# mLSTM scores with queries on the partitions, both directions summed ahead of one value product per block

## The chip, the cores and the metric

The kernel runs on one core of a Trainium2 chip. The metric is the time of one execution in microseconds on the device. The engines are named as in the profile: PE is TensorE (matmuls; PEld are its weight loads), DVE is VectorE, ACT is ScalarE, POOL is GpSimd, and SP is the engine that issues most DMAs.

## The reference

One layer of an encoder block over 512 tokens of width 1024. Three token mixers work side by side on the normed input: a bidirectional mLSTM, a 2-D neighbourhood attention and a cross-attention into a memory. Their outputs are gated, summed and projected, and a gated feed-forward network follows. The change touches the mLSTM alone: 4 heads of width 128, both directions, summed and then normed.

```python
def mlstm_chunkwise(q, k, v, i_pre, f_pre):   # one direction
    ...
    causal = jnp.tril(jnp.ones((L, L), dtype=bool))
    D = a[..., :, None] - a[..., None, :] + log_i[..., None, :]
    D = jnp.where(causal, D, -jnp.inf)
    inter_log = a + m_prev[..., None]
    m_j = jnp.maximum(inter_log, jnp.max(D, axis=-1))
    qk = jnp.einsum('bhcjd,bhcsd->bhcjs', q, k)
    P = jnp.exp(D - m_j[..., None]) * qk
    inter_w = jnp.exp(inter_log - m_j)
    num = jnp.einsum('bhcjs,bhcsd->bhcjd', P, v) + inter_w[..., None] * jnp.einsum('bhcde,bhcje->bhcjd', C_prev, q)
    den = jnp.sum(P, axis=-1) + inter_w * jnp.einsum('bhce,bhcje->bhcj', n_prev, q)
    h = num / jnp.maximum(jnp.abs(den), jnp.exp(-m_j))[..., None]
    return h.reshape(B, H, S, Dh)
...
    h = h_fw + h_bw
    h = h * lax.rsqrt(jnp.mean(h * h, axis=-1, keepdims=True) + EPS)
```

So each direction has its own score matrix `P`, its own denominator and its own inter-block term from the state `C_prev`; the two directions share `qk` and `v`.

## The kernel before

The 512 tokens lie in four blocks of 128 (J = 0 to 3, one chunk of the recurrence each). Weights come from memory as float32 in blocks of 128x1024 (`emit_raw`, on SP's queue, three blocks ahead), are split by ACT (high part, L195) and DVE (low part, L196) into two reduced-precision parts one block ahead (`emit_split`), and each projection is three accumulating matmuls (`mm3`, L213 to L215). A projection of one 128-wide output tile is 24 such passes of 512 columns.

The mLSTM is a generator (`ml_all`, which begins with `ml_prep`) that is stepped in between the projections of other branches: `paced` steps it inside a projection, `step` behind one. `late` holds pieces of work that the next `flush` (in a projection) emits. The order in which instructions then stand on each engine's queue is decided at build time by a scheduler that goes by its own estimates of when inputs are ready; each engine runs its queue in that order.

`ml_prep` computes gates and the running maxima by scans along the tokens, writes one row per head and direction to memory (`rd`) and makes small per-token tables: `bi` and `mh` (exponents), `wt` and `dec` (state weights and decays), `em` (the floor of the denominator), `sc` (the inter-block weight). Per head, `load_R` then loads the two rows back, spread over all partitions (`R`, 128x512 for each direction), `mask` adds the causal mask to them, and the exponential of `R` plus a per-partition column is the decay matrix.

Per head h the stages are:

- `keys`: four transposes of the keys (L681), split into parts; `weigh` multiplies the values by the state weights (L700 to L704).
- `states`: state products of the four blocks (L722 and `mm3`), decayed sums `C` for both directions (L736).
- `edges`: the inter-block term of J = 0 (backward) and J = 3 (forward), which enters as a query scaled by its decay (L673, L675).
- `weights_J`: scores of a block with keys on the partitions (L748), two exponentials (L752), one product `E` for both directions (L753).
- `values_J`, one block later: two value products, one for each direction, with a column of constants in `va` that gives the denominators (L761); for J = 0 and 3 the edge product accumulates into the same PSUM tile (L763), for J = 1 and 2 a 258-wide `mm3` gives the inter-block term of both directions. Then come the denominators (L772 to L779) and the sum of the directions into `H` (L780 to L785), and its squares (L787).
- `normalise`: the power -0.5 on POOL (L793), four scalings by ACT (L798); `emit_y`: four transposes (L806) and the output gate.

The mLSTM stage and what stands beside it end in the merge of the first branch; behind the last transposes of head 3 the cross-attention, the neighbourhood attention, the output projection and the feed-forward network follow.

## Time and profile before

| what | value |
|---|---|
| median of 3 runs | 875.06 us (874.84 to 875.43) |
| the profiled execution's own time | 874.76 us |
| its span, first to last instruction | 873.0 us |
| granted TensorE clock, mean | 0.999 |
| instructions | 12227 |
| first and last key transposes (L681) | 115.7 and 197.4 us |
| last transposes of `emit_y` (L806) | 236.0 us |

In rows of the profile, a line like `L753 DVE TENSOR_TENSOR E<-E,at ...` names the source line, the engine, the operation, and output and inputs by the program's names. In groups, the count is followed by the busy time in us, the mean of one in ns, and the idle time of the engine ahead of it with what ended it. In the timeline the first column is the start and the second the duration, both in us; an idle time ahead of the instruction and its releaser stand in brackets. In windows each engine has its busy time and count, then follow the granted clock, the DMA share and GB/s.

### The profile page before, as it was taken

The page shows a single profiled execution, that of the slowest core. Times are in us where ns is not written, and L with a number is a line of the kernel's source. Part 1 is how long each engine was busy: PE and PEld are TensorE (multiplying, and loading weights), DVE is VectorE, ACT ScalarE, POOL GpSimd, SP SyncE. Part 2 cuts the span into 40 slices and gives each one's busy share as a digit, 9 for nine tenths or more (in the row PEclk, how much of TensorE's full clock was granted, in tenths as well). Part 3 has the DMA queues.
Part 4 walks back from the last instruction along what each step waited for, and adds up shares of the span by engine and source line. Part 5 has one row for each costly group of instructions (what it writes and reads, how often), then busy time and mean ns, then how long its engine had stood idle before and what let it go on. Part 6 is the DMA issues. An engine that isn't in the chain of part 4 may idle for free.

```text
span 873.0 us, 12227 instructions
## 1 busy us (share of the span) xinstructions
PE 867.6 (99%) x4303; PEld 735.9 (84%) x4303; DVE 593.4 (68%) x1240; ACT 470.7 (54%) x996; POOL 125.0 (14%) x201
## 2 busy tenths in 40 slices
PE   9999999999999999999999999999999999999997
PEld 7898889888888888888888888888888888888887
DVE  7794789886577768897676558776633466666534
ACT  7563567765455658898544455444422344444532
POOL 0101100000163370600000002111100011111010
PEclk9999999999999999999999999999999999999999
DMA  8324634522253453633233432332233332322412
GB/s 281 100 79 153 204 122 124 169 82 99 83 143 74 118 151 109 158 121 121 98 97 109 145 108 97 97 97 96 76 100 105 107 98 97 98 96 90 136 40 97
DMA packets 39421, 99.81 MB, mean 114 GB/s; under 512 B 5688, under 2 KB 13880, under 8 KB 39360
## 3 DMA queue, kind: packets, MB, share of 16 engines
q1 hardware_dynamic: 31568, 92.32, 33.3%
q0 software_dynamic: 7360, 6.32, 3.5%
q8 instruction: 34, 0.56, 0.3%
q10 hardware_dynamic: 432, 0.39, 0.1%
q14 instruction: 27, 0.22, 0.1%
HBM read 94.80 MB, written 4.21 MB: 113 GB/s over the span
## 4 chain that ended last, share of the span: by engine, by line
PE 98%; DVE 1%; issue 0%; ACT 0%; POOL 0%; POOLq 0%
PE mm L213 29%; PE mm L214 29%; PE mm L215 29%; PE at L214 2%; PE at L213 2%; PE at L215 2%; PE at L938 1%; PE at L761 1%; PE at L919 1%; PE at L900 0%; PE at L901 0%; PE at L748 0%; PE at L1026 0%; PE at L243 0%; PE mm L422 0%
## 5 line engine op out<-in xcount | busy, mean ns | idle before, releaser
L213 PE MATMUL mm<-u,wh 128*128 128x512 f32 (+1 forms) x1072 | 415.0, 387 | 0.0
L215 PE MATMUL mm<-u,wl 128*128 128x512 f32 (+1 forms) x1072 | 411.8, 384 | 0.0
L214 PE MATMUL mm<-u,wh 128*128 128x512 f32 (+1 forms) x1072 | 411.6, 384 | 0.0
L195 ACT ACTIVATE wh<-wr 128x512 fp32r<-128x512 f32 (+2 forms) x298 | 183.7, 621 | 207.1 <-PE mm L214 163.7
L196 DVE TENSOR_TENSOR wl<-wr,wh 128x512 fp32r<-128x512 f32 (+3 forms) x300 | 203.6, 681 | 89.8 <-ACT wh L195 86.7
L215 PEld LDWEIGHTS mm<-u,wl 128*128 128x128 f32 x1072 | 201.4, 188 | 40.2 <-DVE wl L196 0.2
L213 PEld LDWEIGHTS mm<-u,wh 128*128 128x128 f32 x1072 | 201.5, 188 | 38.6 <-ACT wh L195 0.2
L214 PEld LDWEIGHTS mm<-u,wh 128*128 128x128 f32 x1072 | 201.6, 188 | 38.2
L1374 POOL TENSOR_TENSOR s<-s,rb 128x512 f32<-128x512 f32 x22 | 38.2, 1735 | 402.6 <-DVE s L1373 238.9
L542 POOL DMA_DIRECT2D u<-nav_d x128 | 62.3, 511 | 67.2 <-PE at L938 22.7
L219 ACT ACTIVATE u<-s 128x512 fp32r<-128x512 f32 x26 | 16.4, 632 | 57.9 <-DVE s L1377 56.2
L1377 DVE TENSOR_TENSOR s<-mm,s 128x512 f32<-128x512 f32 x22 | 15.2, 690 | 23.8 <-POOL s L1374 23.8
L462 ACT ACTIVATE s<-pad,vec 128x512 f32<-128x512 f32 x30 | 24.4, 813 | 9.7 <-DVE pad L460 9.7
L220 DVE SCALAR_TENSOR_TENSOR u<-s,u 128x512 fp32r<-128x512 f32 x26 | 19.0, 732 | 14.8 <-ACT u L219 14.7
L463 DVE SCALAR_TENSOR_TENSOR s<-pad,vec,s 128x512 f32<-128x512 f32 x30 | 22.5, 750 | 5.5 <-ACT s L462 5.5
L1373 DVE SCALAR_TENSOR_TENSOR s<-s,s 128x512 f32<-128x512 f32 x22 | 15.2, 691 | 13.4 <-ACT s L1372 13.3
L464 DVE SCALAR_TENSOR_TENSOR s<-pad,vec,s 128x512 f32<-128x512 f32 x30 | 22.5, 750 | 0.8
L1372 ACT ACTIVATE s<-s 128x512 f32<-128x512 f32 x22 | 13.9, 632 | 14.9 <-DVE s L1371 14.9
L460 DVE TENSOR_TENSOR pad<-mm,rb 128x512 f32<-128x512 f32 x22 | 15.1, 690 | 6.5 <-PE mm L215 6.4
L1384 DVE TENSOR_TENSOR u<-mm,u 128x512 f32<-128x512 f32 x13 | 9.0, 691 | 14.6 <-PE mm L215 14.6
L213 PE MATMUL mm<-wh,u 128*128 128x512 f32 x48 | 18.8, 392 | 0.0
L214 PE MATMUL mm<-wl,u 128*128 128x512 f32 x48 | 18.7, 390 | 0.0
(341 smaller groups left out, 1051.5 us busy)
## 6 DMA issues: line engine op xcount, KB each, us to landing
wr<-wflat SPq DMA_DIRECT2D x141, 512.0 KB, 3.4
nab<-nabias SPq DMA_DIRECT2D x16, 256.0 KB, 2.7
u<-nav_d POOLq DMA_DIRECT2D x128, 32.0 KB, 2.8
s<-xT SPq DMA_DIRECT2D x15, 256.0 KB, 4.0
wr<-wflat SPq DMA_DIRECT2D x14, 192.0 KB, 2.4
nav_d<-nv POOLq DMA_DIRECT2D x8, 256.0 KB, 3.7
R<-rd SPq DMA_DIRECT2D x8, 256.0 KB, 5.4
wr<-wflat SPq DMA_DIRECT2D x2, 544.0 KB, 3.4
```

The source lines that it names most:

```text
L195: A.activation(h[:, u:v], src, AF.Copy)
L196: V.tensor_tensor(l[:, u:v], src, h[:, u:v].bitcast(F32), op=ALU.subtract)
L213: PE.matmul(ps, lh, rh, start=start, stop=False)
L214: PE.matmul(ps, lh, rl, start=False, stop=False)
L215: st["mm"] = PE.matmul(ps, ll, rh, start=False, stop=stop).ins
L219: A.activation(h, src, AF.Copy, scale=scale)
L220: V.scalar_tensor_tensor(l, src, scale, h.bitcast(F32), op0=ALU.mult, op1=ALU.subtract)
L462: A.activation(t1, pad[:, 0:512], AF.Identity, scale=vcol(w, i), bias=vcol(b, i))
L463: V.scalar_tensor_tensor(t1, pad[:, 1:513], vcol(w, n + i), t1, op0=ALU.mult, op1=ALU.add)
L464: V.scalar_tensor_tensor(t1, pad[:, 2:514], vcol(w, 2 * n + i), t1, op0=ALU.mult, op1=ALU.add)
L542: G.dma_start(vw[r * 32:(r + 1) * 32, i * 256:(i + 1) * 256], nav_v[hf, r, CW[b]:CW[b] + 32, hp * 256:(hp + 1) * 256])
L1374: G.tensor_tensor(c, c, rb2, op=ALU.mult)
```

## The change

The scores are computed with queries on the partitions, so that a denominator is a column. For each block the two decay matrices are multiplied by the scores with a row sum (`tensor_tensor_reduce`), whose start value is the inter-block part of the denominator; each direction's matrix is then divided by its denominator, the two are added, the sum is transposed on PE and copied to SBUF, and one product with the values follows. The inter-block numerators are scaled and written to `H` ahead of that, and the product is added to them. J = 0 and 3 take their inter-block term from a plain product of the queries with the state, and `edges` is gone. The table `br` replaces `bi` and `mh` in the exponent, `num` holds the two factors that the reciprocals are multiplied by, and the row written to `rd` is another one, which is ready earlier. A block now passes through three steps (`weights_J`, `turn_J`, `values_J`), held in `open_J`; `exps` computes the next block's exponentials at the end of `weights_J`. The key transposes use the projections' PSUM pool. One yield of `ml_prep` goes, and one is added at the end of head 3.

```diff
+        num = cp.tile([P, 2, 2, 4, 4], F32, name="num")
+        with tc.issue_after(st["pool"]):
+            G.memset(num, 1.0 / C_ML)
...
         A.activation(mr[64:100], cu[:36], AF.Copy)
-        yield
         rr = scr()
         rd = dp.tile([2, 4, S], F32, name="rd")
-        yield
-        V.tensor_tensor(rr[:36], cu[:36], mr[:36], op=ALU.subtract)
+        V.tensor_tensor(rr[:36], pl[64:100, :], cu[:36], op=ALU.subtract)
         for d in range(2):
             G.dma_start(rd[d], rr[32 * d:32 * d + 4, :])
+        yield
         yield
...
+            br = cp.tile([P, 2, 4, 4], F32, name="br")
+            sc = [num[:, 1, 0, 1:4], num[:, 1, 1, 0:3]]
             for d in range(2):
...
+                V.tensor_tensor(br[:, d], lfc[:, :, 64 + 32 * d:68 + 32 * d], lfc[:, :, 32 * d:32 * d + 4], op=ALU.subtract)
+                V.tensor_tensor(sc[d], br[:, d, 1 - d:4 - d], mh[:, d:d + 3, d, :], op=ALU.add)
...
-            V.tensor_tensor(r4, r4, msk[d].unsqueeze(1).to_broadcast([P, 4, P]), op=ALU.add)
-
-        def edges(h, R, ee):
-            ...
+            V.tensor_tensor(r4, r4, msk[1 - d].unsqueeze(1).to_broadcast([P, 4, P]), op=ALU.add)
 
         def keys(h, R, ee):
-            pt = atps()
+            pt = mmps()
...
+        def exps(h, J, R):
+            W = tp.tile([P, 4, P], F32, tag="E", name=nm("E"))[:, 0:2, :]
+            for d in range(2):
+                with tc.issue_after(st["act"]):
+                    A.activation(W[:, d, :], R[d][:, J * P:(J + 1) * P], AF.Exp, bias=ml["br"][:, d, J, h:h + 1])
+            ahead.append(W)
+
+        def weights_J(H, ss, h, J, k, w, C, q, R, ee):
+            num, W = ml["num"], ahead.pop()
             js, hs = slice(J * P, (J + 1) * P), slice(h * S + J * P, h * S + (J + 1) * P)
+            ds = (1,) if J == 0 else (0,) if J == NT - 1 else (0, 1)
             ps = atps()
             kq = ps[:, 384:512]
-            PE.matmul(kq, kT[:, hs], qT[:, hs], start=True, stop=True)
+            PE.matmul(kq, qT[:, hs], kT[:, hs], start=True, stop=True)
+            if len(ds) == 2:
+                qs = slice((J - 1) * P, J * P)
+                mm3(ps[:, :258], q[0][:, qs], q[1][:, qs], w[1][J - 1], w[2][J - 1], True, True)
+            else:
+                d = ds[0]
+                PE.matmul(ps[:, 129 * d:129 * d + 129], qT[:, hs], C[d][J - 1 + d], start=True, stop=True)
+            pi = ps[:, :258].rearrange("p (d c) -> p d c", d=2)
+            E = ee[:, J % 2 * 256:J % 2 * 256 + 256].rearrange("p (x c) -> p x c", x=2)
+            y = tiny(8)
+            init, den, r = y[:, 0:2], y[:, 2:4], y[:, 4:8].rearrange("p (x d) -> p x d", x=2)
+            dd = slice(ds[0], ds[-1] + 1)
+            V.tensor_tensor(init[:, dd], pi[:, dd, 128], num[:, 1, dd, J, h], op=ALU.mult)
             for d in range(2):
...
+                V.tensor_tensor_reduce(W[:, d, :], W[:, d, :], kq, C_ML, init[:, d:d + 1] if d in ds else 0.0,
+                                       ALU.mult, ALU.add, accum_out=den[:, d:d + 1])
             emv = em[:, J, :].rearrange("p (a b) -> p a b", b=4)
+            V.scalar_tensor_tensor(den, den, -1.0, den, op0=ALU.mult, op1=ALU.max)
             V.tensor_tensor(den, den, emv[:, 0:9:8, h], op=ALU.max)
             V.reciprocal(den, den)
...
+            V.tensor_tensor(r, num[:, :, :, J, h], den.unsqueeze(1).to_broadcast([P, 2, 2]), op=ALU.mult)
+            A.activation(E[:, 0, :], W[:, 0, :], AF.Copy, scale=r[:, 0, 0:1])
+            V.scalar_tensor_tensor(E[:, 0, :], W[:, 1, :], r[:, 0, 1:2], E[:, 0, :], op0=ALU.mult, op1=ALU.add)
+            src = None
+            for d in ds:
+                if src is None:
+                    A.activation(H[:, js], pi[:, d, 0:128], AF.Copy, scale=r[:, 1, d:d + 1])
+                else:
+                    V.scalar_tensor_tensor(H[:, js], pi[:, d, 0:128], r[:, 1, d:d + 1], src, op0=ALU.mult, op1=ALU.add)
+                src = H[:, js]
+            if J < NT - 1:
+                exps(h, J + 1, R)
+            return H, ss, h, J, E, ps
+
+        def turn_J(H, ss, h, J, E, ps):
+            pt = ps[:, 384:512]
+            PE.transpose(pt, E[:, 0, :], ident)
+            A.activation(E[:, 1, :], pt, AF.Copy)
+
+        def values_J(H, ss, h, J, E, ps):
+            js = slice(J * P, (J + 1) * P)
+            pv = ps[:, 384:512]
+            PE.matmul(pv, E[:, 1, :], va[:, J, h, 0:128], start=True, stop=True)
+            V.tensor_tensor(H[:, js], pv, H[:, js], op=ALU.add)
             sq = scr(128)
             A.activation(sq, H[:, js], AF.Square, accum_out=ss[:, J:J + 1])
...
         for h in range(4):
             if prev:
-                values_J(h - 1, 3, *E, *own, *prev)
-                normalise(*prev)
+                values_J(*open_J.pop(0))
+                turn_J(*open_J[0])
             states(h, *st_h)
...
+            exps(h, 0, R)
+            yield
+            if prev:
+                values_J(*open_J.pop(0))
+                normalise(*prev)
+            last = prev
+            prev = tp.tile([P, S], F32, tag="H", name=nm("H"), bufs=4), tiny(4)
+            open_J.append(weights_J(*prev, h, 0, *own))
             yield
             for J in range(1, NT):
...
+                if J > 1:
+                    values_J(*open_J.pop(0))
+                turn_J(*open_J[0])
+                if J == 2 and last:
+                    emit_y(h - 1, last[0])
+                open_J.append(weights_J(*prev, h, J, *own))
                 if J == 3 and h < 3:
-                    st_h = keys(h + 1, *nxt)
+                    st_h = keyed(h + 1)
+                if J < 3 and h < 3:
+                    late.append(lambda d=J - 1, n=nxt: mask(n, d))
                 yield
...
```

In the built order of the new kernel, `weigh` is at L694 to L698, the state products at L716, the scores at L750, the inter-block product of J = 0 and 3 at L756, the reduce at L764, the scaling at L771 and the combination at L772, the transpose at L786 and its copy at L787, the value product at L792 and the addition at L793, the four scalings of `normalise` at L806, the masks at L670. The norm of the memory (L337 to L341), with two table loads on ACT, and the `o` projections run beside head 0 in both kernels.

More of the change, by code (lines that the diff above doesn't have):

```diff
@@ L615, in ml_prep @@
         em = cp.tile([P, NT, 36], F32, name="em")
-        cp.tile([P, NT, 38], F32, name="gap2")
+        cp.tile([P, NT, 30], F32, name="gap2")
         A.activation(lfc, pmv, AF.Copy)
@@ L708, in keys, with states @@
             late.append(weigh)
-            return (ke, kh, kl), (ew, wh, wl), C, q, eq, R
-        def states(h, k, w, C, q, eq, R):
+            return (ke, kh, kl), (ew, wh, wl), C, q, R, ee
+        def states(h, k, w, C, q, R, ee):
             flush()
@@ L740, in states @@
                 split_act(wh[j], wl[j], tj[j][:, :258])
-        def weights_J(h, J, R):
-            bi = ml["bi"]
+        def exps(h, J, R):
+            W = tp.tile([P, 4, P], F32, tag="E", name=nm("E"))[:, 0:2, :]
+            for d in range(2):
+                with tc.issue_after(st["act"]):
[3 more added lines that the diff above has]
+            num, W = ml["num"], ahead.pop()
@@ L814, in ml_all, with keyed @@
         prev = None
-        E = None
-        def load_head(h):
-            return load_R(h), tp.tile([P, S], F32, tag="H", name=nm("ee"), bufs=4)
-        nxt = load_head(0)
-        st_h = keys(0, *nxt)
+        open_J, ahead = [], []
+        def keyed(h):
+            return keys(h, nxt, tp.tile([P, S], F32, tag="H", name=nm("ee"), bufs=4))
+        nxt = load_R(0)
+        st_h = keyed(0)
         yield
```

70 lines of the change are left out of this document (9 added, 61 removed).

## The prediction

> **What bounds the kernel now.** I read the page first: the busy shares, the slices, the chain that ended last.
>
> ```profile
> span 873.0 us, 12227 instructions
> PE 867.6 (99%) x4303; PEld 735.9 (84%) x4303; DVE 593.4 (68%) x1240; ACT 470.7 (54%) x996; POOL 125.0 (14%) x201
> DVE  7794789886577768897676558776633466666534
> PE 98%; DVE 1%; issue 0%; ACT 0%; POOL 0%; POOLq 0%
> ```
>
> TensorE is the bound from end to end, so the time falls only by passes taken off PE and rises only by waits put into PE's queue. The mLSTM heads run between about 110 and 236 us, interleaved with projections; there DVE is the second busiest, so I looked at that stretch by windows (columns: PE, PEld, DVE, ACT, POOL).
>
> ```profile
> 110.00:120.00 10.00, 10.00 (x52) 8.43 (x51) 9.84 (x32) 6.58 (x17) 1.03 (x2) 1.00 0.24 67
> 120.00:130.00 10.00, 10.00 (x51) 8.45 (x51) 7.43 (x20) 7.43 (x23) 0.00 (x0) 1.00 0.62 199
> 130.00:140.00 10.00, 10.00 (x54) 8.53 (x54) 9.24 (x30) 9.17 (x22) 0.84 (x1) 1.00 0.23 75
> 140.00:150.00 10.00, 10.00 (x78) 9.65 (x77) 9.02 (x28) 6.65 (x18) 0.00 (x0) 1.00 0.54 144
> ```
>
> PE has no hole here, but DVE is busy 35.5 of 40 us: head 0 has little room for more DVE work or for a DVE that waits.
>
> **PE's passes.** Records overlap, so I go by starts in the timeline of PE.
>
> ```profile
> 131.67 0.39 PE L215 MATMUL mm<-u,wl 128*128 128x512 f32 x1
> 131.90 0.38 PE L748 MATMUL at<-u,u 128*128 128x128 f32 x2
> 132.12 0.61 PE L761 MATMUL at<-u,E 128*128 128x129 f32 x4
> 132.56 0.39 PE L763 MATMUL at<-C,ee 128*128 128x129 f32 x2
> 142.24 0.60 PE L681 MATMUL at<-ident,u 128*128 128x128 f32 x4
> 142.68 0.61 PE L761 MATMUL at<-u,E 128*128 128x129 f32 x4
> ```
>
> A 512-wide pass takes 0.23 us (131.67 to 131.90). Plain float32 products are two passes each: L761 is two matmuls and x4 here, 0.44 us to the next start, 0.11 per pass. The four transposes L681 are x4, one pass each, also 0.44. Per head and block the old code has scores (2 passes) and two value products (4); the new has scores (2), one transpose (1), one value product (2). The inter-block products keep their number: the 258-wide triple for J = 1, 2 and one float32 product for J = 0, 3. That is 6 against 5 passes: 16 x 0.11 = **1.78 us off PE**. The built order of PE agrees: summed over its passes, the stretch from the transposes of the running maxima to the last transpose of head 3 is 1.78 us shorter, and everything after it is the same sequence. By "TensorE: Matmul & The Clock Gate", Part 4, in the Trainium skill, a 128x128 transpose costs about 275 ns within a kernel; the records do last 272 ns, but the starts here are 0.11 apart, and by the rule 16 x 0.275 = 4.4 against the 3.55 of the passes dropped would be an estimated loss of 0.85.
>
> **DVE and ACT.** Rows by shape, between 110 and 245 us:
>
> ```profile
> L753 DVE TENSOR_TENSOR E<-E,at 128x256 f32<-128x256 f32 x16 | 6.6, 413 | 1.2 <-PE at L748 1.2
> L781 DVE SCALAR_TENSOR_TENSOR H<-at,y,H 128x128 f32<-128x128 f32 x16 | 5.6, 347 | 3.2 <-ACT H L780 3.1
> L779 DVE RECIPROCAL y<-y 128x2 f32<-128x2 f32 x16 | 2.6, 161 | 0.3
> L327 DVE CUSTOM_DVE_ANT_0 s<-at,ident 128x128 f32<-128x128 f32 x2 | 0.6, 282 | 0.0
> L327 DVE DVE_READ_ACCUMULATOR2_ANT y<- 128x1 f32 x2 | 0.2, 82 | 0.0
> ```
>
> Per head DVE loses four L753 (1.65), eight H updates (2.78), fourteen tiny operations at about 0.16 (2.2) and the edge product (about 0.41): 7.0. It gains eight multiply-and-reduce pairs (8 x 0.364 = 2.9), twenty tiny ones (3.2), six 128-wide combinations (2.1) and four additions, between a tiny 0.16 and 0.35, say 0.28 (1.1): 9.3. So +2.3 per head, 9 in all, and about 3 in the four windows above: 38.5 of 40. That fits, just. ACT loses two edge exponentials and four tiny Abs per head and gains four scaled copies and four PSUM copies, about +1. None of this is on PE's path by itself; what counts is the path from a block's scores to its transpose. Before, one DVE product lay between scores and values. Now it is: reduce, reduce, four tiny operations each waiting for the last, an ACT scaling, a DVE combination, transpose, an ACT copy, value product. PE is in order, so every wait of these stops the projection passes queued behind it. The built order gives four places where I find the product late.
>
> **Wait 1: R ahead of the state weights.** The rows that become R are now finished right after the scans.
>
> ```profile
> 109.23 1.21 DVE L601 TENSOR_TENSOR_SCAN cu<-on,s 4x512 f32<-4x512 f32 x1
> 115.45 0.68 DVE L607 TENSOR_TENSOR s<-cu,s 36x512 f32<-36x512 f32 x1
> 116.06 0.68 DVE L196 TENSOR_TENSOR wl<-wr,wh 128x512 fp32r<-128x512 f32 x1
> 118.19 0.33 SPq L660 DMA_DIRECT2D R<-rd  x1
> DMA to landing us min/median/max: 4.0/5.4/5.6
> 119.46 0.29 DVE L700 TENSOR_SCALAR s<-u,wt 128x129 f32<-128x129 f32 x1
> 122.08 0.38 PE L722 MATMUL at<-s 128*128 128x129 f32 x2
> 122.21 0.40 ACT L673 ACTIVATE ee<-R,mt 128x128 f32<-128x128 f32 x1 [0.85 <-DMA R<-rd]
> 124.29 0.40 ACT L673 ACTIVATE ee<-R,mt 128x128 f32<-128x128 f32 x1 [1.67 <-DMA R<-rd]
> ```
>
> From the end of L607 (116.13) to the first R issue are 2.06 us, then 4.0 to 5.6 to landing. In the new order the scans end at 110.44 as before, one split follows, then the subtraction, which ends near 111.75; so R is issued at 113.8 and lands at 117.8 to 119.4, about four microseconds sooner than now. But the masks move up in DVE's queue further than that. The first one stands behind four 512-wide operations (0.60 each from start to start, 115.45 to 116.06), eight 256-wide ones (0.41 each by L753) and a few tiny ones, 5.9 us: DVE is there at 117.6 and waits 0.2 to 1.8 for R. Queued behind it are a 256-wide subtraction, the copy of mt, the second mask, eight tiny operations, a weight split and the third mask (0.41 + 0.2 + 0.6 + 0.65 + 0.6 + 0.6), and only then L694, the old L700 (0.29). With the first mask's own 0.6 that is 3.95, some 3.8 with overlaps, after R's landing: 121.6 to 123.2. In the built order PE has five 512-wide passes fewer ahead of its first state product (old L722): 122.08 - 5 x 0.23 = 120.95. The wait is 0.65 to 2.25; I take **1.2**, nearer to the 4.0 us landing, since that one was also the first of its batch. The split behind the masks is wanted by PE only around 126 and stays covered. In the old order L700 was 2.6 us ahead of L722 and no mask stood before it.
>
> **Waits 2 and 3: blocks 2 and 3 of head 0.**
>
> ```profile
> 131.29 1.28 ACT L337 ACT_TABLE_LOAD   x1
> 132.98 1.28 ACT L1092 ACT_TABLE_LOAD   x1
> 134.81 0.40 ACT L338 ACTIVATE s<-s 128x256 f32<-128x256 f32 x1
> 135.28 0.42 DVE L339 SCALAR_TENSOR_TENSOR s<-at,s 128x256 f32<-128x256 f32 x1
> 136.71 0.15 DVE L778 TENSOR_TENSOR y<-y,em 128x2 f32<-128x2 f32 x1
> 139.34 0.80 SPq L660 DMA_DIRECT2D R<-rd  x2
> ```
>
> Two table loads for the memory norm now stand on ACT between block 0's copy and block 1's scaling and behind it (load, L337, two scalings, load, L338). Behind the first state product PE has 34 passes of 512, ten of 256 columns and ten float32 ones to the transpose of block 0 (7.7 + 1.2 + 1.1): 131.0, with wait 1 132.2. ACT then has a tanh, the copy and an exponential (about 1.3) and the five operations with two loads (2.56 + 0.41 + 0.7): the second load ends near 137.3, L338 near 137.7. DVE's L339 waits for it, and behind L339 in DVE's queue stands all of block 2: the norm's own operations (1.43, from 135.28 to 136.71), two weight splits and two operations of the o projection (2.2), a mask of head 2's R (0.6), the reduces of blocks 2 and 3, an addition and the tiny ones (about 2.4): 6.6 us, so block 2's combination ends near 144.3. PE's transpose of it is 37 passes of 512, three of 256 and sixteen float32 ones on (10.5): 142.7, and the projection passes behind it wait with it. The mask can lengthen this: R for head 2 is issued after the last exponential of block 3, near 138.1 (139.34 before), and lands at 142.1 to 143.7, where DVE gets to the mask near 142.4. Wait 0 (if the norm's part overlaps) to 2.5, taken **1.3**; block 3 is next in the same queue, 0 to 0.7, **0.4**. By "ScalarE: Activation LUTs", What ACT_TABLE_LOAD costs, in the Trainium skill, a load is 1.28 us plus a drain of 1.38; here 0.41 lie between the end of the first (132.57) and the start of the second, with L337 in them, so no drain shows; with drains the wait would be an estimated 2.8 longer.
>
> **Wait 4: head 0's norm ahead of head 1's first block.**
>
> ```profile
> 152.45 0.31 ACT L787 ACTIVATE s<-H 128x128 f32<-128x128 f32 x1 [0.42 <-DVE H L781]
> 152.52 0.28 PE L213 MATMUL mm<-u,wh 128*128 128x256 f32 x1
> 152.88 0.28 PE L213 MATMUL mm<-u,wh 128*128 128x256 f32 x1
> 154.18 1.28 ACT L798 ACTIVATE H<-H,y 128x128 f32<-128x128 f32 x4 [0.70 <-POOL y L793]
> 155.36 0.40 ACT L219 ACTIVATE u<-C 128x258 fp32r<-128x258 f32 x1
> ```
>
> From the last square to the operation behind the four scalings are 2.91 us (152.45 to 155.36), with GpSimd's power inside. In the new ACT queue the scaling of the next head's block 0 stands right behind these four. The chain from head 0's last value product is: 0.75 to the square (a pass, an addition, hand-overs; my estimate from 0.38 for two passes and 0.28), 2.91, in head 1 also a split on ACT and one on DVE (0.8 in all), the scaling 0.32, the combination 0.35: 5.1. PE has between the two points eight float32 passes and 29 of 256 columns (three in 0.36 us, 152.52 to 152.88): 0.9 + 3.5 = 4.4. Wait 0 to 1.2, taken 0.7 plus a hand-over, **0.8**. In heads 2 and 3 no split lies between, and PE has six float32 passes and 18 of 512 columns: a chain of 4.3 against 4.8, covered.
>
> **What costs nothing.** GpSimd's memset of num stands among its other early memsets, and GpSimd is 14% busy. The R loads stay eight; that of head 2 waits on SP's queue ahead of a weight load, but weights are loaded three blocks (of 5 us) ahead; without that cover it would be the 4 to 5.6 us of a landing. Block tiles stay open over three steps instead of two, which with the states' two makes four, just the pool; a fifth would wait for one addition, under 0.3. That the key transposes move to the projections' PSUM pool frees one there for each pair of inter-block products that leaves it.
>
> **The sum.** The other blocks have 4 to 6 us of PE work between scores and transpose against a chain of some 2.5, covered by projections. 1.2 + 1.3 + 0.4 + 0.8 = 3.7 of waits, minus 1.78: **+1.9 us**. The profiled execution took 874.76 (span 873.0 and 1.76 around it), so 876.7; the median of the three runs is 0.30 above it, so **877.0** against 875.06. Own range of this case: all waits at half, 875.1, to all at the upper ends (2.25 + 2.5 + 0.7 + 1.2), 879.9, and 880.5 with small ones in other blocks.
>
> **Rivals.** (a) *The covers hold: faster.* The first R lands before DVE reaches the mask at 117.5 and the table loads are absorbed. It decides at R's landing in 3.7 us or less and a chain of block 2 that is 1.5 shorter; with waits under 0.1 in sum the full 1.78 stays: 873.3, and 873.0 with the runs' spread of 0.3. For it: PE shows no wait at all now, though ACT waited 0.85 and 1.67 for the same R; against it: no R landed in under 4.0. 0.2. (b) *Half covered.* Wait 1 and 4 at their low ends, 2 and 3 partly: waits of 0.1 to 3.5, 873.4 to 876.8. 0.3. (c) *My forecast*, waits of 3.5 to 7: 0.4. (d) *DVE becomes the bound in head 0*: if the 3 us added cannot overlap, weight splits come late as well and PE follows DVE from 110 to 155; 38.5 of 40 plus 3 to 5 us of its own waits is 2 to 4 over, on top of wait 4: 879 to 882. 0.07. (e) *The transpose costs PE its record's 0.27*, not 0.11, by the mechanism that a lone transpose between 512-wide passes isn't overlapped; 16 x 0.16 = 2.6 more, 879.6 with the waits. 0.03, as the four in a row overlap. This is what the rule of the Trainium skill quoted above (TensorE: Matmul & The Clock Gate) amounts to. That the change does not drop the passes is excluded by the built order.
>
> **Numbers.** Two tenths of a per cent (1.75 us) is about what a measurement of this kernel tells from no change. Faster: (a), 0.2. Same: (b), 0.3, 873.31 to 876.81. Slower: (c) to (e), 0.5. The range 873.0 to 880.5 goes from (a) to the upper end of (c).
>
> **What would show it.** Right: PE's matmul records fall by 16; gaps on PE ahead of the first state product (about 121), the transposes of blocks 2 and 3 (143 to 148) and of head 1's block 0 (about 158); DVE's first mask waiting for R; L339 waiting for ACT beyond 137. Wrong: no gap over 0.3 there (then (a)), or DVE without idle time from 110 to 155 (then (d)).

## The result and the profile after

The changed kernel takes 880.07 us (median of four runs, 878.94 to 880.92) against 875.17 (874.84 to 875.43) for the kernel before on the same chip: a ratio of 1.0055, 95% interval 1.0038 to 1.0073. It is slower, by about 4.9 us. The four runs lie in two pairs, 878.94 and 879.32, and 880.82 and 880.92; the profiled one belongs to the upper pair. What parts them is explained below; no run lies at the median itself, so differences from 880.07 are some 0.8 to 1.1 off for either pair, and sizes are better read from the stretches in the table further down.

The page of the changed kernel, with the waits of PE from the view of waits behind it (time in total, how often, the longest):

```profile
span 879.1 us, 12264 instructions
PE 869.4 (99%) x4287; PEld 734.7 (84%) x4287; DVE 598.3 (68%) x1316; ACT 476.4 (54%) x1005; POOL 125.1 (14%) x202
PE 92%; DVE 3%; ACT 2%; DMA 2%; issue 1%; POOL 0%; SPq 0%; POOLq 0%; DVEq 0%
PE at L716 <- DVE s L694: 1.9, 1, 1.9
PE at L786 <- DVE H L778: 1.2, 2, 1.0
PE at L786 <- ACT wh L195: 1.0, 1, 1.0
```

PE has 16 records fewer (4287 for 4303), as it should, and is yet busy 1.8 us longer. The chain that ended last was 98% PE and is 92% now: DVE, ACT and a DMA have come onto it, at three places. The same four windows as before:

```profile
110.00:120.00 10.00, 10.00 (x51) 8.30 (x50) 8.28 (x20) 5.93 (x13) 1.03 (x2) 1.00 0.48 125
120.00:130.00 10.00, 8.07 (x35) 6.69 (x35) 8.33 (x28) 6.64 (x22) 0.00 (x0) 0.83 0.27 89
130.00:140.00 10.00, 10.00 (x52) 8.00 (x51) 8.59 (x37) 8.21 (x19) 0.00 (x0) 1.00 0.32 106
140.00:150.00 10.00, 9.03 (x50) 7.46 (x49) 9.07 (x38) 7.13 (x23) 0.84 (x1) 1.00 0.46 107
```

PE loses 1.93 us from 120 to 130 and 0.97 from 140 to 150. DVE is not fuller than before (34.3 of 40 us against 35.5): it waits more. And in the second window the granted clock is 0.83, which no window before showed.

All of the loss lies in one stretch. From the start of the transposes of the gates' logarithms (L583) to that of the last transposes of `emit_y` the timeline of PE gives, and from there the start of its last pass lies 632.0 to 632.1 us later in each of these kernels:

| kernel | from | to | stretch | against before |
|---|---|---|---|---|
| before | 104.02 | 236.02 | 132.00 | |
| changed | 104.31 | 242.17 | 137.86 | +5.86 |
| masks moved | 104.36 | 237.26 | 132.90 | +0.90 |
| no table loads | 104.99 | 239.93 | 134.94 | +2.94 |
| scalings moved | 104.23 | 239.24 | 135.01 | +3.01 |
| masks and scalings moved | 104.76 | 236.39 | 131.63 | -0.37 |
| the same, with L632 on ACT and L685 later | 104.71 | 238.13 | 133.42 | +1.42 |
| masks, scalings and two splits moved | 104.73 | 235.74 | 131.01 | -0.99 |

**The first state product.** Rows of the timelines of DVE, POOL, SP and PE of the changed kernel; after them one row of its DMA view and the same of the kernel before (x, KB each, median us to landing):

```profile
111.49 0.69 DVE L608 TENSOR_TENSOR s<-at,cu 36x512 f32<-36x512 f32 x1
112.48 1.03 POOL L610 DMA_DIRECT2D rd<-s  x2 [14.87 <-DVE s L608]
115.26 1.76 SPq L664 DMA_DIRECT2D R<-rd  x4
119.60 0.69 DVE L670 TENSOR_TENSOR R<-R,msk 128x512 f32<-128x512 f32 x1 [1.63 <-DMA R<-rd]
123.07 0.29 DVE L694 TENSOR_SCALAR s<-u,wt 128x129 f32<-128x129 f32 x1
121.18 0.39 PE L213 MATMUL mm<-u,wh 128*128 128x512 f32 x1
123.50 0.71 PE L716 MATMUL at<-s 128*128 128x129 f32 x2 [1.93 <-DVE s L694]
124.44 0.63 PE L214 MATMUL mm<-u,wh 128*128 128x512 f32 x1
124.86 0.63 PE L215 MATMUL mm<-u,wl 128*128 128x512 f32 x1
rd<-s POOLq DMA_DIRECT2D x2, 8.0 KB, 2.6
```

```profile
rd<-s POOLq DMA_DIRECT2D x2, 8.0 KB, 1.7
```

DVE's first mask stands idle 1.63 us for R; the state weights (L694) are behind it in the queue, and PE behind those. From start to start PE loses 123.50 - 121.18 - 0.23 = 2.09 us. And then comes something that was not forecast: the next 512-wide passes start 0.42 apart (124.44, 124.86) instead of 0.23, up to about 127. In sum the starts from 120 to 130 us come 3.8 later than their passes cost, so this is 1.7 more.

**Block 2 of head 0, and block 0 of head 1.** Rows of ACT, DVE, POOL and PE:

```profile
136.61 1.28 ACT L337 ACT_TABLE_LOAD   x1
138.86 1.28 ACT L338 ACT_TABLE_LOAD   x1
140.15 0.42 ACT L338 ACTIVATE s<-s 128x256 f32<-128x256 f32 x1
140.60 0.43 DVE L339 SCALAR_TENSOR_TENSOR s<-at,s 128x256 f32<-128x256 f32 x1 [1.37 <-ACT s L338]
145.27 0.69 DVE L670 TENSOR_TENSOR R<-R,msk 128x512 f32<-128x512 f32 x1 [0.20 <-DMA R<-rd]
146.76 0.35 DVE L772 SCALAR_TENSOR_TENSOR ee<-E,y,ee 128x128 f32<-128x128 f32 x1
146.07 0.39 PE L215 MATMUL mm<-u,wl 128*128 128x512 f32 x1
147.43 0.33 PE L786 MATMUL at<-ident,ee 128*128 128x128 f32 x1 [0.97 <-DVE H L778]
157.95 1.01 POOL L801 TENSOR_TENSOR y<-y,nhalf 128x4 f32<-128x4 f32 x1 [15.25 <-DVE y L762]
158.99 1.29 ACT L806 ACTIVATE H<-H,y 128x128 f32<-128x128 f32 x4 [1.37 <-POOL y L801]
160.71 0.39 ACT L771 ACTIVATE ee<-E,y 128x128 f32<-128x128 f32 x1
160.62 0.28 PE L214 MATMUL mm<-u,wh 128*128 128x256 f32 x1
161.94 0.30 PE L786 MATMUL at<-ident,ee 128*128 128x128 f32 x1 [1.04 <-ACT wh L195]
```

L339 waits 1.37 for ACT, the mask of head 2's R another 0.20 for its DMA, and block 2's combination (L772) ends at 147.1: PE loses 147.43 - 146.07 - 0.23 = 1.13 us, and 0.2 at block 3. For head 1 the power and the four scalings stand before the scaling of its block 0, and a weight split of 0.5 us too (ACT is free of L806 at 160.2 and begins L771 at 160.71): 161.94 - 160.62 - 0.12 = 1.20. One more, 0.42, lies at head 2's block 1 (192.3). Together 2.09 + 1.7 + 1.13 + 0.2 + 1.20 + 0.42 = 6.7; less 1.78 for the passes 5.0; the other 0.9 of the 5.86 are starts late by less than 0.2 each.

### The profile page after: what moved, and what is told of

The parts are those of the page before. It is cut to its first block, busy times and chain, and to the rows that moved or that the text cites. A ratio compares the mean times of both kernels' runs of the same rounds, so it can differ in the third digit from the quotient of the medians.

```text
span 879.1 us, 12264 instructions
## 1 busy us (share of the span) xinstructions
PE 869.4 (99%) x4287; PEld 734.7 (84%) x4287; DVE 598.3 (68%) x1316; ACT 476.4 (54%) x1005; POOL 125.1 (14%) x202
## 4 chain that ended last, share of the span: by engine, by line
PE 92%; DVE 3%; ACT 2%; DMA 2%; issue 1%; POOL 0%; SPq 0%; POOLq 0%; DVEq 0%
PE mm L215 27%; PE mm L213 27%; PE mm L214 27%; PE at L214 2%; PE at L213 2%; PE at L215 2%; DMA R<-rd 1%; PE at L953 1%; PE at L934 1%; PE at L915 0%; DVE wl L196 0%; PE at L916 0%; DMA wr<-wflat 0%; ACT wh L195 0%; PE at L1041 0%
## 5 line engine op out<-in xcount | busy, mean ns | idle before, releaser
L214 PEld LDWEIGHTS mm<-u,wh 128*128 128x128 f32 x1072 | 202.0, 188 | 38.5
L462 ACT ACTIVATE s<-pad,vec 128x512 f32<-128x512 f32 x30 | 24.5, 816 | 9.8 <-DVE pad L460 9.8
L1167 DVE TENSOR_TENSOR s<-mm,rb_x 128x512 f32<-128x512 f32 x16 | 11.0, 689 | 12.1 <-PE mm L215 12.1
```

What stands on the lines that cost most here:

```text
L214: PE.matmul(ps, lh, rl, start=False, stop=False)
L462: A.activation(t1, pad[:, 0:512], AF.Identity, scale=vcol(w, i), bias=vcol(b, i))
```

## Experiments

The theory: the new time is the old one less 1.78 us of passes, plus separate waits of PE, each with its own chain. The main rival: DVE is simply full in head 0, so that any wait taken away comes back as another.

**The masks behind the state weights.** The masks of heads 0 and 1 go behind `weigh` in DVE's queue:

```diff
+                with tc.issue_after(st["dve"]):
                     for d in range(2):
                         mask(R, d)
...
+                        with tc.issue_after(st["dve"]):
+                            mask(n, d)
```

> The four masks of heads 0 and 1 are queued on DVE behind the state weights (L694 to L698); nothing else is edited. Theory (the new time is the old one less 1.78 us of passes plus separate waits of PE, and the one at the first state product comes from the masks standing ahead of the weights while R is still under way): the 2.1 us gap ahead of L716 goes below 0.3, the granted clock stays at 1.0 behind it, and the time falls by 2.1 to 3.8 us against the changed kernel, to 876.3 to 878.0. The gaps at the transposes of block 2 (1.1) and of head 1's block 0 (1.2) stay. Rival (DVE is simply full in head 0, so an order of its queue only moves the wait): PE waits as long somewhere between 121 and 135 us, time 879.5 to 880.5.

876.26 us (11 runs, 875.97 to 876.68), ratio to the kernel before 1.0009 (1.0001 to 1.0018): 3.8 below the changed kernel, just under the expected range. From the timelines of DVE and PE:

```profile
120.02 0.29 DVE L694 TENSOR_SCALAR s<-u,wt 128x129 f32<-128x129 f32 x1 [0.22 <-ACT wt L647]
120.46 0.46 PE L716 MATMUL at<-s 128*128 128x129 f32 x2 [0.43 <-DVE s L694]
```

L694 starts three microseconds earlier and PE's gap is 0.59 (the pass before started at 119.64), not the 0.3 that was expected. No pass behind it is slow. Head 1's wait stays (0.99), but that of block 2 is gone as well, which was not expected. The scheduler has moved other work along: PE comes to block 2's transpose 7.5 us after the end of the second table load (135.91 to 143.4; in the changed kernel 6.2, 140.14 to 146.3), and the mask of head 2's R stands behind block 2's chain. So the 3.8 us are not all the first wait's: of the 4.96 between the two stretches in the table 1.5 are that wait, 1.7 the slow passes behind it, 1.3 blocks 2 and 3, the rest small ones.

**No table loads.** The memory's norm with a copy in place of its logarithm:

```diff
-        A.activation(v, ps[:, :ntok], AF.Ln, scale=1.0 / n)
+        A.activation(v, ps[:, :ntok], AF.Copy if tag == "m" else AF.Ln, scale=1.0 / n)
```

> The logarithm in the memory's norm is replaced by a copy, which leaves out the logarithm there, so that ACT need not change its tables twice between 136 and 140 us. Theory (separate waits): L339 on DVE no longer waits 1.4 us for ACT, the gaps ahead of the transposes of blocks 2 and 3 of head 0 (1.1 and 0.2) go below 0.3 together, the time falls by 1.0 to 1.4 against the changed kernel, to 878.7 to 879.1; the gap at the first state product stays at 2.1. Rival (block 2 is late because DVE's queue is long, whatever ACT does): the gap stays over 0.8, time within 0.4 of 880.1.

878.79 us (878.60 to 879.75), 1.0042 (1.0028 to 1.0056), within the expected range. L339 no longer waits, and block 2's transpose follows its predecessors without a gap:

```profile
136.97 0.41 DVE L339 SCALAR_TENSOR_TENSOR s<-at,s 128x256 f32<-128x256 f32 x1
147.14 0.39 PE L716 MATMUL at<-s 128*128 128x129 f32 x2
147.37 0.27 PE L786 MATMUL at<-ident,ee 128*128 128x128 f32 x1
145.54 0.67 DVE L670 TENSOR_TENSOR R<-R,msk 128x512 f32<-128x512 f32 x1
```

The gap at the first state product stays (2.10). The stretch is 2.92 shorter than the changed kernel's: 1.7 are the slow passes, which this profile does not have, and 1.2 the gaps at blocks 2 and 3. (In times the pairs blur this: three runs at 878.6 to 878.8 and two at 879.7, so the lower group is only some 0.4 below the changed kernel's lower one, the upper 1.2 below its upper one.) But the order moved too: the mask of head 2's R, within block 2's chain in the changed kernel, starts at 145.54 here, behind block 2's combination (143.22). So the run shows that the wait at block 2 goes when L339's wait and the mask are both out of its way, and not that the table loads alone made it.

**The scalings behind the next head's block 0.**

```diff
+            st["e0"] = A.activation(E[:, 0, :], W[:, 0, :], AF.Copy, scale=r[:, 0, 0:1]).ins
...
+                with tc.issue_after(st["e0"]):
                     for J in range(NT):
                         ...
                         A.activation(H[:, js], H[:, js], AF.Copy, scale=rs[:, J:J + 1])
```

> The four scalings of a finished head (L806) are queued on ACT behind the scaling of the next head's block 0 (L771). Theory (the power on GpSimd and the four scalings hold up head 1's block 0): the 1.2 us gap ahead of the transpose of head 1's block 0 goes below 0.3, time 878.6 to 879.2. Rival (block 0 of head 1 is late by its own DVE chain, and ACT's queue only looks like the cause since it comes last): the gap shrinks by less than 0.5, time 879.6 to 880.2.

878.06 us (877.66 to 879.99), 1.0032 (1.0020 to 1.0045), 0.5 under the expected range, since four of its five runs lie in the lower group; against the changed kernel's lower group it is some 1.0 less. On ACT the order is now L771 and then the scalings (L807 here), and PE's gap at head 1's block 0 is 159.17 - 158.91 - 0.11 = 0.15:

```profile
158.24 0.40 ACT L771 ACTIVATE ee<-E,y 128x128 f32<-128x128 f32 x1 [0.83 <-DVE y L770]
158.79 1.27 ACT L807 ACTIVATE H<-H,y 128x128 f32<-128x128 f32 x4
159.17 0.30 PE L786 MATMUL at<-ident,ee 128*128 128x128 f32 x1
```

A new gap of 0.62 stands at the transpose at 172.9 us, head 1's block 2 (the next expectation but one puts it down to head 2), and that of head 2's block 1 (0.42) has gone: small waits move with this change of order.

**All three, with the power on GpSimd.** Masks and scalings moved, and the memory's norm as one scaling on DVE and one power on GpSimd over 128x256.

```diff
+        if tag == "m":
+            V.tensor_scalar(v, ps[:, :ntok], 1.0 / n, None, op0=ALU.mult)
+            G.tensor_tensor(rb, v, nhalf[:, 0:1].to_broadcast([P, ntok]), op=ALU.pow)
+            return rb
         A.activation(v, ps[:, :ntok], AF.Ln, scale=1.0 / n)
```

> The masks behind the state weights, the scalings behind the next block 0, and the memory's norm by one DVE scaling and one power on GpSimd in place of logarithm, exponential and Newton step. Theory (waits add up and are all that stands between the two kernels): PE is left with the 1.78 us it lost in passes and about 0.4 of small waits, time 873.3 to 874.2, faster than both kernels. Rival (a wait that is removed uncovers the next one in the queues, DVE 38.5 of 40 us busy): 875 to 877.5. The power over 128x256 has no row so far; if GpSimd takes over 6 us for it, the keys and values of the memory wait for the norm and the time is above 876.

902.68 us (901.82 to 902.81), 1.0308 (1.0294 to 1.0322). The rival's condition on GpSimd holds, by far. From POOL's timeline and the waits of PE:

```profile
132.81 41.16 POOL L339 TENSOR_TENSOR rb_m<-s,nhalf 128x256 f32<-128x256 f32 x1 [19.01 <-DVE y L772]
PE mm L215 <- DVE wl L196: 24.5, 1, 24.5
```

The projection that needs the norm stands in DVE's queue ahead of a weight split, and PE stops for 24.5 us. On the theory this run says nothing.

**Masks and scalings alone.** The two edits with `issue_after` from above, together.

> The masks behind the state weights and the four scalings behind the next block 0, without the GpSimd power that cost 41 us. Theory (separate waits, each worth its own gap): against the run with the masks alone (876.26) the 1.0 us gap ahead of the transpose of head 1's block 0 goes, 875.2 to 875.4; with the 0.6 that appeared ahead of head 2's block 0 when the scalings alone were moved, up to 875.9. Rival (a removed wait uncovers the next in DVE's queue in full): 876.0 to 876.5.

874.96 us (11 runs, 874.59 to 875.50), 0.9997 (0.9988 to 1.0006): 1.3 below the masks alone (1.1 when each is set against its own runs of the kernel before), a little under the expected 875.2. In the waits of PE one line of the heads is left:

```profile
PE at L716 <- DVE s L694: 0.4, 1, 0.4
```

The gap at head 1's block 0 went from 0.98 to 0.24, and the 0.42 at head 2's block 1, which was not expected to, went too; no wait came in their place, as separate waits would have it. But the kernel only draws level with the one before.

**L632 and L685.** As the last, with the copy of the spread maxima on ACT and the low part of the keys behind the small tables.

```diff
-            V.tensor_copy(mt.rearrange("p d t x h -> p (d t x h)"), pt[:, :64])
+            A.activation(mt.rearrange("p d t x h -> p (d t x h)"), pt[:, :64], AF.Copy)
...
+            low = lambda: V.tensor_tensor(kl, pt[:, P:3 * P], kh.bitcast(F32), op=ALU.subtract)
...
+                if h == 0:
+                    with tc.issue_after(st["tab"]):
+                        low()
```

> As the run with masks and scalings moved, and in head 0 the copy of the spread maxima (L632) by ACT in place of DVE and the low part of the keys (L685) computed behind the small tables, so that DVE comes to the state weights earlier. Theory: of the 0.6 us that PE still waits ahead of the first state product 0.4 to 0.6 go, 0.4 to 0.6 below the run before it: 874.6 to 875.4. If ACT's copy comes late for the tables (rival), the gap stays at 0.6 and the time with it.

876.69 us (875.99 to 876.97), 1.0016 (1.0007 to 1.0025): a miss. The first gap only went from 0.58 to 0.47, the wait at block 2 came back (1.23), and one of 0.50 is new at head 1's block 2. Rows of DVE and PE (lines are five further on here):

```profile
137.27 0.43 DVE L339 SCALAR_TENSOR_TENSOR s<-at,s 128x256 f32<-128x256 f32 x1 [1.37 <-ACT s L338]
142.01 0.69 DVE L670 TENSOR_TENSOR R<-R,msk 128x512 f32<-128x512 f32 x1 [0.28 <-DMA R<-rd]
144.16 0.33 PE L791 MATMUL at<-ident,ee 128*128 128x128 f32 x1 [1.07 <-DVE H L783]
```

The new order is that of the changed kernel again: L339 waits for the second table load, and the mask of head 2's R, with its own wait, stands within block 2's chain. In the traces of the new order, the one with the long power aside, the two come together and PE waits 0.81 to 1.23 at block 2 (the changed kernel twice, the scalings alone, this run), or neither does and it does not wait (the other five). So no run says how much is the norm's and how much the mask's; it hangs on where the scheduler puts them.

**Two weight splits behind the state weights as well.** Masks and scalings moved, and the low parts of the weight block that PE wants only from about 124 us on.

```diff
+                with (tc.issue_after(st["hold"]) if "hold" in st else contextlib.nullcontext()):
                     V.tensor_tensor(l[:, u:v], src, h[:, u:v].bitcast(F32), op=ALU.subtract)
...
+                if h == 0:
+                    st["hold"] = st["dve"]
```

> As the run with masks and scalings moved, and the low parts of one weight block (two L196 of 0.6 us, wanted by PE only from about 124 us on) are queued on DVE behind the state weights as well. Theory: DVE reaches the state weights 1.2 us earlier, the 0.6 us that PE still waits ahead of the first state product goes, 874.2 to 874.6, under the kernel before by about 0.8. Rival (the gate chain itself, from the transposes of the maxima to the tables, is late): the gap stays over 0.4, 874.8 to 875.2; or an order that shifts again puts a wait of 1 us at block 2 of head 0, as in the run before: 875.5 to 876.5.

874.36 us (11 runs, 874.01 to 875.10), 0.9992 (0.9983 to 1.0001). The first gap is gone (the state product is L724 here; the pass ahead of it started at 119.34), and the view of waits has no line of the heads any more (the largest late start left is 0.24, at head 1's block 0). With no long waits left DVE's own load shows in the windows:

```profile
119.65 0.46 PE L724 MATMUL at<-s 128*128 128x129 f32 x2
sum 40.00, PE 40.00 PEld 34.12 DVE 38.15 ACT 32.22 POOL 1.86; mean PE 10.00 PEld 8.53 DVE 9.54 ACT 8.05 POOL 0.47
```

DVE is busy 38.15 of the 40 us from 110 to 150, and PE 40.00: it fits. The same kernel again:

> The version with masks, scalings and two splits moved, once more, since its ratio to the kernel before had an interval that just touches one. Theory (1.78 us of passes less, about 0.65 of small waits more in the stretch of the heads): the same 0.6 to 1.1 us under the kernel before. Rival (the difference was the chip's spread of one session): within 0.3 us of it.

874.33 us (11 runs, 873.84 to 874.85) beside 875.37, 0.9987 (0.9978 to 0.9996). The interval of the first session just touches one, that of the second does not: this version is faster than the kernel before by 0.7 to 1.0 us, and than the change as it was made by some 5.6 to 5.9 by the medians.

**The changed kernel again, and the clock.** Four runs on the slow passes behind the first state product.

> The changed kernel itself once more. Theory: the 2.1 us wait ahead of the first state product stands just where the clock falls or does not, so the times lie in two groups 1.6 us apart, 878.9 to 879.5 and 880.6 to 881.2, whose profiles differ in the passes between 124 and 128 us. Rival: the two groups come from something else, and a profile of the low group shows a shorter wait there.

Five runs: 878.48, 878.78, 879.15, 879.36 and 881.55; 1.0043 (1.0030 to 1.0057). Two groups again, but the profiled upper run had a longer wait too (2.57), so this alone doesn't part the theories. Over all kernels that keep a wait of 2.1 or more there, 6 of 19 runs are in an upper group, 1 to 3 us above the others, and each run's mean granted clock parts them the same way: 0.997 or 0.998 in those six, 0.999 or 1.000 in the other 13. Half the clock for some 3.4 us is 0.002 of the span, so the groups go with the clock. Of the 55 runs of the kernels with the masks moved (the one with the long power aside) none is over 1.1 us above the fastest of its session, though one run of the kernel before, which has no long wait, was 1.6 above (876.51, at 0.999). Then a ladder of waits, put into PE's queue of the kernel before, ahead of the down projections:

```diff
+            if f > 0:
+                t = [scr(), scr()]
+                V.tensor_copy(t[0], last_ps)
+                for n in range(f - 1):
+                    V.tensor_copy(t[1 - n % 2], t[n % 2])
+                gate = PE.transpose(atps()[:, :P], t[(f - 1) % 2][:, :P], ident).ins
```

> The kernel before, with waits put into PE's queue in the feed-forward's down projections: ahead of each one PE transposes the end of a chain of DVE copies (128x512) that starts with the product before. The chain has 1 to 7 copies in the first half and 1 to 4 in the second; between two waits PE has about 7.5 us of passes. At 0.35 to 0.6 us per copy the waits go from 0.8 to about 4 us, the time to 895 to 903. Theory (a wait of some 2 us makes the granted clock fall to half for about 3.3 us behind it): behind waits over 2 us passes start 0.42 us apart for 3 us and then 0.23 again, behind waits up to 1.2 us none does. Rival (the half clock behind the first state product in the changed kernel has another cause than the length of the wait): passes stay 0.23 apart behind waits of 2 to 3 us.

936.19 us: each chain stood behind an addition and a weight split on DVE, so the waits were 2.23 to 5.00 us, 38.9 in all, which is why the time was missed. Behind ten of the eleven waits the passes are slow, 1.5 to 2.7 us in sum; behind one of 2.70 none is, though both of 2.23 have them. Length alone does not decide. Two more, with other chains:

```diff
+            c = V.tensor_copy(t[0], ps).ins
+            for n in range(f % 3):
+                with tc.issue_after(c):
+                    c = V.tensor_copy(t[1 - n % 2], t[n % 2]).ins
+            gate = PE.transpose(atps()[:, :P], t[f % 3 % 2][:, :P], ident).ins
```

> The kernel before with waits in PE's queue ahead of the feed-forward's down projections, shorter than in the first ladder: chains of one, two or three DVE copies in turn that begin as soon as a product ends, waits of about 1.0, 2.1 and 2.5 us. Theory (a wait of about 2 us lies where the granted clock may or may not fall, a wait of about 1 us never makes it fall): no passes at 0.42 behind the waits of 1.0, behind some of those of 2.1 and 2.5 and not behind others. Rival (a fixed threshold just above 2 us): all of 2.5 and none of 2.1. Time 875 plus some 20 us of waits plus 1.6 for each fall: 895 to 908.

```diff
+                V.tensor_copy(t[:, :512], last_ps[:, :512])
+                gate = PE.transpose(atps()[:, :P], t[:, :P], ident).ins
```

> The same with one copy each time that stands behind the addition and a weight split on DVE, so that all eleven waits are about 2.2 us, as long as the one at the first state product in the changed kernel. Theory (whether the clock falls depends on when the wait lies, not on its length alone): passes at 0.42 us behind some of the eleven and not behind others, as in two of four runs of the changed kernel. Rival (length alone decides): behind all or none. Time 875 plus 24 of waits plus 1.6 for each fall: 899 to 918.

899.32 and 906.55 us. Waits of 0.94 (five of them), 1.97 (two) and 2.27 have no slow pass behind them, two waits of 2.43 have, one of 2.53 has not, which puts out a fixed threshold. Of the eleven equal waits, three have. Two of those eleven in PE's timeline, from the transpose that waits (the idle time in brackets counts from the end of the record ahead, the 2.23 from 0.23 us after that pass's start):

```profile
647.07 0.30 PE L1385 MATMUL at<-ident,s 128*128 128x128 f32 x1 [2.07 <-DVE s L1384]
647.60 0.63 PE L214 MATMUL mm<-u,wh 128*128 128x512 f32 x1
648.02 0.63 PE L215 MATMUL mm<-u,wl 128*128 128x512 f32 x1
658.54 0.30 PE L1385 MATMUL at<-ident,s 128*128 128x128 f32 x1 [2.08 <-DVE s L1384]
658.91 0.40 PE L214 MATMUL mm<-u,wh 128*128 128x512 f32 x1
659.15 0.40 PE L215 MATMUL mm<-u,wl 128*128 128x512 f32 x1
```

The granted clock in windows behind them:

```profile
647.25:650.66 3.41, 3.41 (x10) 2.64 (x10) 0.00 (x0) 0.00 (x0) 0.00 (x0) 0.50 0.00 0
658.60:662.60 4.00, 4.00 (x19) 3.29 (x20) 0.51 (x1) 0.63 (x1) 0.00 (x0) 1.00 0.02 4
```

The same wait of 2.23 us costs 1.6 more in one place and nothing in the other. The places have a rule, and the trace's record of the granted clock dates it. In this trace the clock is at half from 637.01, 647.25 and 688.21 on, for 3.413 us each; the starts are 10.24 and 40.96 apart, 3 and 12 times 3.413. In all three traces every stretch at half clock lasts one such step or two, and starts a whole number of steps from the others. So within a trace the time falls into cells of 3.413 us, and the clock is set cell by cell. The cells laid over the eleven waits (a wait from the end of the pass's 0.23 to the transpose's start):

| wait from | most of it in one cell, us | slow passes behind it |
|---|---|---|
| 633.31 | 1.95 | yes |
| 644.84 | 2.23 | yes |
| 656.31 | 1.18 | no |
| 666.22 | 1.51 | no |
| 676.04 | 1.92 | no |
| 685.93 | 2.23 | yes |
| 697.43 | 1.22 | no |
| 834.48 | 1.73 | no |
| 844.38 | 1.40 | no |
| 854.29 | 1.17 | no |
| 864.20 | 1.50 | no |

All 33 waits of the three traces part at about 2 us within one cell: up to 1.92 none has slow passes behind it, from 2.08 on each has, and of the three at 1.95, 1.97 and 2.00 the first and the last have. The slow stretch is the cell that follows. The kernels with the wait at the first state product bear it out, their cells dated by the half clock in the last microseconds of each execution: the two profiles of the changed kernel have 2.09 and 2.08 us of it in one cell and slow passes behind it, the runs without table loads and with the scalings moved have 1.52 and 1.87 in one cell, of waits as long (2.10 and 2.08), and none. So the length of the wait and its place decide together.

## Why the prediction was right, and where not

Direction and range were right: slower, forecast 877.0 in 873.0 to 880.5, measured 880.07. The size was short by 3.1 us, and that the median lies within the range is in part luck: the pair of runs at 878.94 and 879.32 does, the pair at 880.82 and 880.92 lies above it, by a loss that the sum had no term for.

- **The passes, -1.78.** Right. Five passes for six: 16 records fewer; with all late starts taken off, at 0.11 for a pass of 128 columns and 0.23 for one of 512, the stretches in the table leave a gain of 1.8 us in each of the seven kernels (this checks that the waits add up, more than the price itself). Rival (e) is out: from a transpose L786 to the pass after the next it takes 0.11 to 0.18 us more than the pass between them costs, 0.13 on average, and not 0.27. (The next 512-wide pass starts as little as 0.03 behind the transpose, but the one behind that then comes 0.31 later instead of 0.23.) By the Trainium skill (TensorE: Matmul & The Clock Gate, Part 4) a 128x128 transpose (in bf16) takes about 275 ns within a kernel; the trace shows that as the record of these float32 ones, and about half of it on PE's path.
- **Wait 1, forecast 1.2, measured 2.09 and in some runs 1.7 more.** The mechanism was right to the order of the queue: DVE idle ahead of the first mask, then 3.5 us from the mask's start to L694 and its 0.29 on top, for the 3.8 forecast. The mis-sized term is the way of the rows through memory. L608 ended at 112.18 instead of 111.75, the rows' store took 2.6 to land instead of the 1.7 that was built into the 2.06 taken from the old trace, so R was issued at 115.26 instead of 113.8 and landed at 119.6, just past the forecast's upper end of 119.4. In the three other traces with this order the store took 2.1 to 2.4 us and R's load 4.6 to 5.3 (4.3 here); from the end of L608 to the first mask it is 7.4 to 7.9 us in all four, and the 1.2 had left room for some 6.6 (111.75 to about 118.35).
- **The granted clock was no term of the sum.** The trace of before had no wait of PE over 0.8 us, so it could show nothing of it; that no price was set on a wait's consequence for PE itself is the step that was missing. By the rows above a wait of 2.1 to 2.2 us costs 1.5 to 1.7 more about one time in three. The Trainium skill (TensorE: Matmul & The Clock Gate, Part 1) says that the clock is judged in a free-running window of 3413 ns and drops after an idle one: the steps of 3.413 agree. Its advice there ("Why this matters for your kernels") to keep idle gaps under some 3 us does not: some 2 us inside one window were enough.
- **Waits 2 and 3, forecast 1.3 and 0.4, measured 1.13 and 0.2.** Right, with the chain as forecast: table loads, L338, L339 waiting beyond 137, then the mask of head 2's R and block 2. How much of it is the norm's and how much the mask's is not shown, since they came and went together. The times were 2.5 to 3 us later than forecast (L338 at 140.15, not 137.7), as all behind wait 1.
- **Wait 4, forecast 0.8, measured 1.20.** Power and scalings as forecast, and shown by the run that moves the scalings. PE's work in between was as forecast (4.38 for 4.4); the chain of 5.1 took 5.58, from the value product at 156.36 to the transpose at 161.94: 0.86 to the square for 0.75, 2.97 from there to the operation behind the scalings for 2.91, and 1.75 for the two splits, the scaling and the combination, which had 1.47.
- **"Covered" heads 2 and 3.** Nearly: one wait of 0.42 at head 2's block 1, not foreseen.
- **Rivals.** Covers that hold (a) and half covers (b) are out by the waits. The median lies in the band of (d), DVE as the bound, but that is not its cause: with the masks, scalings and two splits in another order PE has no wait over 0.25 while DVE does the same work, 38.15 of 40 us, where 38.5 was forecast. DVE's growth over the whole kernel was sized wrongly, 9 us forecast and 598.3 - 593.4 = 4.9 measured; nothing hung on it.

What stays open: the remaining starts late by under 0.2 us each, about 0.9 us in the changed kernel, were not traced, nor why R's load took 5.3 us in the one profile with a wait of 2.57.

## What to carry to other kernels

When a product's path gets longer, look at what the scheduler puts between the new steps: here the arithmetic was a gain of 1.78 us, and four queue orders, of masks, table loads, scalings and weight splits, turned it into a loss of 4.9; queuing masks, scalings and two splits behind the critical work gave back 5.6 to 5.9. A wait that is wanted by PE costs more than itself if it may reach about 2 us, so price that too. Fixing one order by hand moves others: read the built order and the waits again after each.

## What the runs showed of the hardware

- The granted clock falls to half for 3.41 us, one cell of a fixed grid of 3.413 us, when PE has been idle for about 2 us or more within the cell before: behind none of 17 waits with up to 1.92 us in one cell, two of three at 1.95 to 2.00, each of 13 from 2.08 on. A cell at half clock cost 1.5 to 1.7 us; four waits of 3.3 to 4.1 us ran on into it by 1.0 to 1.9, and the clock stayed down for two cells, 2.3 to 2.7 us.
- A lone 128x128 transpose between passes cost PE 0.11 to 0.18 us, where its record lasts 0.27 to 0.33.
- A power on GpSimd over 128x256 took 41.16 us, 0.16 per column; the one over 128x4 takes 1.01.
- Two small stores by GpSimd's queue landed in 2.1 to 2.6 us in ten traces of the new order; four microseconds later in the execution, in four traces of the old one, they took 1.7.
